# A two-layer hybrid decoder on one core: the compressions' first layer with activations stationary on four column groups

## The chip, the core and the metric
The kernel runs on one NeuronCore of a Trainium2 chip. The metric is the time of one execution in microseconds (us) on the device, everything included from the first load to the last store. Engines are named as the profile names them: PE (TensorE's matmuls), PEld (its weight loads), DVE (VectorE), ACT (ScalarE), POOL (GpSimd) and SP (SyncE, which here only issues DMAs).

## The reference
Two layers run one after the other on 512 tokens of width 1024. Each layer is a half-step SwiGLU, a mixer, a second half-step SwiGLU and a gated input embedding, with layer norms between. The mixer holds three kinds of attention heads side by side. The change is inside one of them, the sparse attention's compression of keys and values:

```python
def compress(kv, pe, w1, w2):
    blk = kv[:, idx] + pe[:, None, :]
    blk = jnp.transpose(blk, (0, 1, 3, 2, 4)).reshape(B, n_cmp, NSA_KV_HEADS, CMP_BLOCK * HEAD_DIM)
    return jax.nn.gelu(blk @ w1) @ w2
```

There are 31 blocks (padded to 32 in the kernel) of 32 tokens by 64 channels, so `blk` is 32 by 2048 and `w1` is 2048 by 256. It is done once for keys and once for values in each layer: four times in all. All of it is float32.

## The kernel before
Big products are made in three passes of a reduced float32 (fp32r): each operand is split into a high part (`whi`, `xh`) and a low part (`wlo`, `xl`), and high by high, low by high and high by low are added in PSUM. A 128x1024 chunk of weights is a "unit": SP loads it as `raw`, ACT copies the high part, DVE or POOL subtracts to get the low part (`_split`, L209 to L219).

The mixer (`mixer`, L423) is written as a list of steps, `SEQ`, of projections (G, q0, q1, kk), score and softmax steps (Q), transposes of the probabilities (T) and products with the values (P). A scheduling layer then places each engine's instructions. So each engine has a fixed order, and an instruction waits only for what it needs.

The steps `cmp`, `hk0` to `hk3`, `hv0` to `hv3`, `ck`, `cv`, `cs`, `ct` are the compression. `g_cmp` (L608) makes `xs`: for keys and for values a tile of 128 partitions, 16 slices of the 2048 inputs and 32 blocks. `phi(i, j)` (L623) is step `hk`j (i = 0) or `hv`j (i = 1); it takes one unit of weights, `wraw`, unsplit, which holds four slices of 128 inputs by 256 outputs. These weights are plain float32. For each slice and each half of the outputs, the weights are the stationary operand (128 columns) and the 32 blocks of `xs` move:

```python
for b in range(4):
    k = 4 * j + b
    for m in range(2):
        self.mm(p[:, 32 * m:32 * m + 32], w[:, b, m], M["X"][:, i, k], k + m == 0, k == 15, True)
```

The result of 16 slices is a 128x64 piece of a PSUM bank `ps` of tag "g". There are two banks of that tag. The bank is taken at j = 0 and is held until DVE has copied it to `gx` (L636). After that come the gelu on DVE (L639 to L647, with one exponential on ACT, L643) and the second layer, `cmp_k` (L653) or `cmp_v`. All matrix products are issued by the helper `mm`, so they all stand at line L249 in the profile; rows are told apart by their tiles. The softmaxes' scores go through two banks of tag "s", and DVE reads each at L732, which is the step that frees the bank.

Of the kernel before, what the change touches and what calls it, by code (L numbers as in the profile page):

```python
# [19 lines left out]
F32 = mybir.dt.float32  # L20
F32R = mybir.dt.float32r
AF = mybir.ActivationFunctionType
# [29 lines left out]
def _mix(w, n):  # L52

    return w.reshape(-1, n, 2, 64 // n).transpose(0, 2, 3, 1).reshape(-1, 128)
# [61 lines left out]
def _consts():  # L116
    c = {}
    c["ident"] = np.eye(128, dtype=np.float32)
    q = np.arange(128)
    m = np.zeros((128, 512), np.float32)  # L120
    m[:, 384:] = np.where(q[None, :] <= q[:, None], 0.0, NEG)
    c["mask"] = m
    ut = np.ones((128, 512), np.float32)
    ut[:, :128] = (q[:, None] <= q[None, :])
    c["ut"] = ut

    def table(d, pos):
        inv = (np.float32(10000.0) ** (-np.arange(0, d, 2, dtype=np.float32) / np.float32(d))).astype(np.float32)
        ang = pos.astype(np.float32)[:, None] * inv[None, :]
        co, si = np.cos(ang).astype(np.float32), np.sin(ang).astype(np.float32)  # L130
        n = 128 // d
        return [np.ascontiguousarray(_mix(np.tile(np.concatenate(x, 1), (1, n)), n).T)
                for x in ((co, co), (-si, si))]

    t = np.arange(S)
    c["rope"] = np.stack([*table(64, t), *table(32, t)])
    be = np.arange(32) * 16 + 31
    c["ropec"] = np.stack(table(64, be), 1)
    ok = (np.arange(32)[None, :] < NCMP) & (be[None, :] <= t[:, None])
    c["maskc"] = np.where(ok, 0.0, NEG).astype(np.float32).reshape(4, 128, 32).transpose(1, 0, 2)  # L140
    c["rowc"] = (t >= 31).astype(np.float32).reshape(4, 128).T
    b = np.zeros((128, 128), np.float32)
    b[:64, :64] = b[64:, 64:] = 1.0 / 64
    c["bd"] = b
    return {k: np.ascontiguousarray(v, np.float32) for k, v in c.items()}


def layout(a):

    a = {k: np.asarray(v) for k, v in a.items()}  # L150
    o = dict(_consts())
    o["x"] = a["x"][0]
    o["xt"] = a["x"][0].T.reshape(KC, 128, S).transpose(1, 0, 2)
    o["pt"] = a["p"][:, 0].transpose(0, 2, 1).reshape(L, 2, 128, S).transpose(0, 2, 1, 3)
    o["ws"] = np.stack(_stream(a, 0) + _stream(a, 1))
    o["ln_g"], o["ln_b"], o["bg"] = a["ln_g"], a["ln_b"], a["ple_b_gate"]
    k2 = a["nsa_phi_k2"].reshape(L, 2, 128, 2, 32)
    o["phik2"] = np.stack([np.repeat(x.reshape(L, 2, 128, 64), 2, 3) for x in (k2, k2[..., ::-1, :])], 3).transpose(0, 2, 1, 3, 4)
    o["phiv2"] = a["nsa_phi_v2"].reshape(L, 2, 128, 64).transpose(0, 2, 1, 3)
    o["pe"] = np.stack([a["nsa_pos_k"], a["nsa_pos_v"]], 1).reshape(L, 2, 16, 128).transpose(0, 3, 1, 2)  # L160
    o["bf"] = a["fox_b_f"]
    o["lam"] = a["diff_lambda"].reshape(L, 128)
    o["sg"] = np.concatenate([a["diff_subln_g"]] * 2, 1)
    return {k: np.ascontiguousarray(v) for k, v in o.items()}
# [3 lines left out]
class _Body:  # L168
# [78 lines left out]
    def mm(self, out, l, r, start, stop, loose=False):  # L247

        self.nc.tensor.matmul(out, l, r, start=start, stop=stop, skip_group_check=loose)  # L249
# [176 lines left out]
    def mixer(self, l):  # L426
        nc, A = self.nc, self.A
# [18 lines left out]
        M = {}  # L446
# [21 lines left out]
        for t in range(NT):  # L468
            p = self.ps("gs"[t % 2])
# [153 lines left out]
        def phi(i, j):  # L623

            if j == 0:
                M["ps", i] = self.ps("g")
            p = M["ps", i][:, 0:64]
            w = self.unit().rearrange("p (b m n) -> p b m n", b=4, m=2)
            for b in range(4):
                k = 4 * j + b  # L630
                for m in range(2):
                    self.mm(p[:, 32 * m:32 * m + 32], w[:, b, m], M["X"][:, i, k], k + m == 0, k == 15, True)
            if j < 3:
                return
            x, y = lw([128, 2, 32], f"gx{i}"), lw([128, 2, 32], f"gy{i}")
            nc.vector.tensor_copy(x, p.rearrange("p (a b) -> p a b", a=2))  # L636

            c = 2.0 * math.sqrt(2.0 / math.pi)
            nc.vector.tensor_mul(y, x, x)  # L639
            nc.vector.tensor_scalar(y, y, -0.044715 * c, -c, op0=ALU.mult, op1=ALU.add)  # L640
            nc.vector.tensor_mul(y, y, x)
            nc.vector.tensor_scalar(y, y, 80.0, None, op0=ALU.min)
            nc.scalar.activation(y, y, AF.Exp)  # L643
            nc.vector.tensor_scalar(y, y, 1.0, None, op0=ALU.add)  # L644
            nc.vector.reciprocal(y, y)
            if i == 0:
                nc.vector.tensor_mul(x, x, y)  # L647
                M["phi", 0] = x
            else:
                g = M["phi", 1] = lw([128, 2, 4, 32], "g1")  # L650
                nc.vector.tensor_mul(g, *(a[:, :, None, :].to_broadcast([128, 2, 4, 32]) for a in (x, y)))
# [225 lines left out]
        for n in SEQ:  # L877
            if n[0] == "h":
                phi("kv".index(n[1]), int(n[2]))
            elif n in steps:  # L880
                steps[n]()
                if len(M) and all(k in M for k in (("q", 0), ("q", 1), "k")) and "n0" not in M:
                    ready()
            else:
                {"G": G, "Q": QS, "T": TP, "P": PV}[n[0]](n[1:])
# [21 lines left out]
        g, b = self.bcast(A["ln_g"][l, 1]), self.bcast(A["ln_b"][l, 1])  # L907
# [55 lines left out]
    def start(self):  # L963
        nc, A = self.nc, self.A

        self.ident = self.cp.tile([128, 128], F32, name="ident")
        self.mhalf = self.cp.tile([128, 1], F32, name="mhalf")
        self.one = self.cp.tile([128, 1], F32, name="one")
        self.eps = self.cp.tile([128, 1], F32, name="eps")
        for n in ("mask", "bd", "maskc", "rowc", "ropec"):  # L970
            setattr(self, n, self.cp.tile(list(A[n].shape), F32, name=n))
        self.xh = self.cp.tile([128, KC, S], F32R, name="xh")
        self.xl = self.cp.tile([128, KC, S], F32R, name="xl")
        nc.vector.memset(self.mhalf, -0.5)
        self.x = [self.h4(F32, name="x") for t in range(NT)]

        z = self.h4(shape=(128, 512), name="zero")
        nc.vector.memset(z.bitcast(F32), 0.0)
        p = self.ps("t")
        for _ in range(self.opt["warm"]):  # L980
            self.mm(p, z[:, 0:128], z, True, True)

        raw = [self.h4(F32, name="raw") for _ in range(2)]
        for u in range(2):
            self.hl[u] = [self.big(self.tags[u], name="w") for _ in range(2)]
        for k in range(KC):
            r = self.big("h", F32, (128, 512), "xraw")
            x = nc.sync.dma_start(r, A["xt"][:, k])
            if k % 2 == 0:
                c = slice(128 * k, 128 * k + 256)  # L990
                for u in range(2):
                    self.last_raw = nc.sync.dma_start(raw[u][:, c], A["ws"][u, :, c])
            self.hilo(self.xh[:, k], self.xl[:, k], r)
            if k % 2 == 0:
                for u in range(2):
                    self.hilo(self.hl[u][0][:, c], self.hl[u][1][:, c], raw[u][:, c])
        self.dma_u = self.split_u = 2
        for u in range(2, 4):
            self._load(u)
            self.after(self.last_raw, x)  # L1000
            self.dma_u += 1
        self.ahead(3)
        nc.vector.memset(self.one, 1.0)
        nc.vector.memset(self.eps, EPS)

    def load_x(self):
        nc, A = self.nc, self.A
        for t, n in ((self.ident, A["ident"]), *((self.x[t], A["x"][128 * t:128 * t + 128]) for t in range(NT)),
                     *((getattr(self, n), A[n]) for n in ("mask", "bd", "maskc", "rowc", "ropec"))):
            self.after(nc.sync.dma_start(t, n), self.last_raw)  # L1010


# [71 lines left out]
```

## Time and profile before

| what | us |
|---|---|
| median of 3 runs | 2188.41 |
| lowest and highest run | 2184.15, 2189.64 |
| the profiled execution, its own time | 2182.96 |
| its span, first to last instruction | 2181.1 |
| PE busy | 2138.7 (98%) |
| PEld busy | 1765.9 (81%) |
| DVE busy | 1049.2 (48%) |
| ACT busy | 819.6 (38%) |
| POOL busy | 152.5 (7%) |

A line of the profile reads: start, duration, engine, line of the kernel, operation, tiles written and read, `rows*columns` of the array, shape, count. Matmuls overlap in a pipeline, so what one costs is the distance from its start to the next one's start, and not its duration. A float32 matmul with no split appears as two MATMUL and two LDWEIGHTS records; one of fp32r as one of each.

### The profile page before, as it was taken

To read this page: it belongs to the slowest core of one execution; us is meant where nothing else is said; L and a number is where in the kernel's file an instruction comes from. 1 tells how busy PE (TensorE), PEld (TensorE's weight loads), DVE (VectorE), ACT (ScalarE), POOL (GpSimd) and SP (SyncE) were. 2 spreads that over 40 slices of the span, in tenths; PEclk is the share of its full clock that TensorE was granted. 3 is DMA by queue.
4 is the path that set the end of the run, shared out by engine and by line. 5 is a ranking of instruction groups with operands and counts; after the bars stand their busy time and mean duration, and the time that the engine had idled before them with its cause. 6 is when DMAs were issued, how large, how long until landed. Compare 5 with 4: busy or idle time off the path is not lost.

```text
span 2181.1 us, 25953 instructions
## 1 busy us (share of the span) xinstructions
PE 2138.7 (98%) x10135; PEld 1765.9 (81%) x10135; DVE 1049.2 (48%) x1777; ACT 819.6 (38%) x1372; POOL 152.5 (7%) x114
## 2 busy tenths in 40 slices
PE   9999999999999999999999999999998999999999
PEld 7888888787778888887888888887877788888887
DVE  4333236378875333334723332363788753333355
ACT  5222213456763222213522222144577532222132
POOL 0000001212210000000000000012212200000000
PEclk9999999989999999999999999999999999999999
DMA  6323334432342323334313333344323413333332
GB/s 202 97 97 97 108 105 152 128 127 92 104 145 66 97 97 97 116 96 136 97 59 97 97 97 106 107 143 136 122 92 110 152 51 96 98 97 118 94 134 68
DMA packets 76107, 236.07 MB, mean 108 GB/s; under 512 B 11344, under 2 KB 13520, under 8 KB 75984
## 3 DMA queue, kind: packets, MB, share of 16 engines
q1 hardware_dynamic: 74864, 230.74, 33.5%
q0 software_dynamic: 1120, 3.67, 0.5%
q8 instruction: 80, 1.31, 0.2%
q14 instruction: 43, 0.35, 0.1%
HBM read 209.46 MB, written 6.29 MB: 99 GB/s over the span
## 4 chain that ended last, share of the span: by engine, by line
PE 89%; DVE 6%; ACT 2%; DMA 1%; issue 1%; SPq 0%; DVEq 0%; ACTq 0%
PE ps L249 86%; PE ps L756 2%; PE ps L266 1%; DMA raw<-in_ws_dram 1%; DVE P L746 1%; DVE P L732 1%; ACT whi L218 1%; DVE PT L242 0%; DVE P L742 0%; DVE wlo L219 0%; DVE raw_r L540 0%; DVE gy L644 0%; DVE pair L797 0%; DMA xraw<-in_xt_dram 0%; DVE xl L269 0%
## 5 line engine op out<-in xcount | busy, mean ns | idle before, releaser
L218 ACT ACTIVATE whi<-raw 128x1024 fp32r<-128x1024 f32 x342 | 361.7, 1060 | 1047.5 <-PE ps L249 678.5
L219 DVE TENSOR_TENSOR wlo<-raw,whi 128x1024 fp32r<-128x1024 f32 x298 | 363.8, 1223 | 609.4 <-ACT whi L218 609.0
L249 PE MATMUL ps<-xh,wlo 128*128 128x512 f32 (+1 forms) x1688 | 644.7, 382 | 0.1
L249 PE MATMUL ps<-xl,whi 128*128 128x512 f32 (+1 forms) x1688 | 644.5, 382 | 0.0
L249 PE MATMUL ps<-xh,whi 128*128 128x512 f32 (+1 forms) x1688 | 643.5, 382 | 0.8 <-ACT xh L268 0.8
L249 PE MATMUL ps<-whi,h 128*128 128x512 f32 x1376 | 430.2, 392 | 0.0
L249 PEld LDWEIGHTS ps<-xh,whi 128*128 128x128 f32 x1688 | 317.2, 188 | 59.9 <-ACT xh L268 1.5
L249 PEld LDWEIGHTS ps<-xh,wlo 128*128 128x128 f32 x1688 | 318.0, 188 | 58.7 <-DVE wlo L219 0.5
L249 PEld LDWEIGHTS ps<-xl,whi 128*128 128x128 f32 x1688 | 317.8, 188 | 58.7 <-DVE xl L269 0.6
L249 PEld LDWEIGHTS ps<-whi,h 128*128 128x128 f32 x1376 | 257.9, 188 | 59.1 <-issue 6.9
L249 PE MATMUL ps<-wlo,h 128*128 128x512 f32 (+1 forms) x704 | 277.5, 394 | 0.0
L335 DVE TENSOR_TENSOR hraw<-silu,ps 128x512 f32<-128x512 f32 x88 | 60.5, 687 | 290.7 <-PE ps L249 289.9
L249 PEld LDWEIGHTS ps<-wlo,h 128*128 128x128 f32 (+1 forms) x704 | 132.0, 188 | 35.3 <-issue 9.6
L219 POOL TENSOR_TENSOR wlo<-raw,whi 128x1024 fp32r<-128x1024 f32 x44 | 107.2, 2437 | 286.2 <-ACT whi L218 208.7
L734 ACT ACTIVATE P<-P,sst 128x128 f32<-128x128 f32 x192 | 106.6, 559 | 26.4 <-DVE sst L732 26.0
L249 PE MATMUL ps<-whi,xh 128*128 128x512 f32 (+2 forms) x264 | 98.9, 377 | 2.0 <-DVE VF L466 2.0
L298 POOL TENSOR_TENSOR mv<-mv,mhalf 128x1 f32<-128x1 f32 x24 | 23.0, 957 | 1111.3 <-DVE mv L297 1111.3
L732 DVE CUSTOM_DVE_ANT_0 P<-ps,mask 128x128 f32<-128x128 f32 x192 | 90.1, 490 | 21.7 <-PE ps L249 20.7
L249 PE MATMUL ps<-wlo,xh 128*128 128x512 f32 (+2 forms) x264 | 98.8, 375 | 0.0
L249 PE MATMUL ps<-whi,xl 128*128 128x512 f32 (+2 forms) x264 | 98.3, 374 | 0.0
L756 PE MATMUL ps<-ident,P 128*128 128x128 f32 x400 | 71.2, 297 | 12.9 <-DVE P L746 9.4
L249 PE MATMUL ps<-whi,oT 128*128 128x512 f32 x256 | 82.6, 395 | 0.0
(194 smaller groups left out, 1928.7 us busy)
## 6 DMA issues: line engine op xcount, KB each, us to landing
raw<-in_ws_dram SPq DMA_DIRECT2D x342, 512.0 KB
wraw<-in_ws_dram SPq DMA_DIRECT2D x16, 512.0 KB
dx<-x SPq DMA_DIRECT2D x8, 512.0 KB
x<-dx SPq DMA_DIRECT2D x8, 512.0 KB
rot<-raw_r SPq DMA_DIRECT2D x28, 128.0 KB
bc<-in_ln_g_dram SPq DMA_DIRECT2D x6, 512.0 KB
bc<-in_ln_b_dram SPq DMA_DIRECT2D x6, 512.0 KB
xraw<-in_xt_dram SPq DMA_DIRECT2D x8, 256.0 KB
```

The lines of the kernel that those rows point to most:

```text
L218: self.nc.scalar.activation(hi, r, AF.Copy)
L219: (self.nc.gpsimd if self.opt["pool"] and tag[1:] else self.nc.vector).tensor_sub(lo, r, hi.bitcast(F32))
L249: self.nc.tensor.matmul(out, l, r, start=start, stop=stop, skip_group_check=loose)
L266: nc.tensor.transpose(p[:, j], self.x[t][:, 128 * k:128 * k + 128], self.ident)
L298: nc.gpsimd.tensor_tensor(mv[:, 3:4], mv[:, 2:3], self.mhalf, op=ALU.pow)
L335: nc.vector.tensor_mul(r[0:n], s[up:up + n], pu[up:up + n])
L732: nc.vector.tensor_tensor_reduce(v, p[:, 0:n], self.mask[:, 512 - n:512], -scale, 3e38, ALU.add, ALU.min, nm[:, t:t + 1])
L734: nc.scalar.activation(v, v, AF.Exp, bias=nm[:, t:t + 1], scale=-1.0, accum_out=sm[:, t:t + 1])
L746: nc.vector.scalar_tensor_tensor(v, v, r[:, t:t + 1], c, op0=ALU.mult, op1=ALU.add)
L756: nc.tensor.transpose(p[:, 128 * i:128 * i + 128], P[:, off[t] + 128 * kb:off[t] + 128 * kb + 128], self.ident)
```

## The change
In `phi`, the operands change places. The 32 blocks of one slice are now the stationary operand (32 columns), and the slice's 128x256 weights move. The four slices of a unit write four groups of 32 PSUM partitions of the same bank, so each uses its own 32 columns of the array. After the last unit there are four partial sums, each 32 blocks by 256 outputs, on top of each other. ACT copies them to SBUF (`qs`), and two float32 matmuls with `four` (four stacked 32x32 identities) as the moving operand add them and turn them to outputs by blocks. From there on, everything is as before. A constant of 128x32 is added and loaded once with the others.

```diff
+    c["four"] = np.tile(np.eye(32, dtype=np.float32), (4, 1))
...
-            p = M["ps", i][:, 0:64]
-            w = self.unit().rearrange("p (b m n) -> p b m n", b=4, m=2)
+            q = M["ps", i][:, 0:256]
+            w = self.unit().rearrange("p (b n) -> p b n", b=4)
+
             for b in range(4):
-                k = 4 * j + b
-                for m in range(2):
-                    self.mm(p[:, 32 * m:32 * m + 32], w[:, b, m], M["X"][:, i, k], k + m == 0, k == 15, True)
+                self.mm(q[32 * b:32 * b + 32], M["X"][:, i, 4 * j + b], w[:, b], j == 0, j == 3, True)
             if j < 3:
                 return
+
+            qs = self.tmp(shape=(128, 256), name="qs")
+            nc.scalar.activation(qs, q, AF.Copy)
+            p = M["ps", i][:, 256:320]
+            for m in range(2):
+                self.mm(p[:, 32 * m:32 * m + 32], qs[:, 128 * m:128 * m + 128], self.four, m == 0, m == 1, True)
             x, y = lw([128, 2, 32], f"gx{i}"), lw([128, 2, 32], f"gy{i}")
...
+        self.four = self.cp.tile([128, 32], F32, name="four")
```

The scheduling layer also moves instructions around these. Lines below the change stand 1 or 6 lines further down in the new program (L249 is L250, L636 is L642).

On PE, where the first units of the keys' compression stand between other heads' work (`ident,P` is a transpose of probabilities, `fb,fa` scores, `PT,VF` a product with values), the order before is:

```order
L249 MATMUL ps<-xs,wraw 128x32 x8
L756 MATMUL ps<-ident,P 128x128 x10
L249 MATMUL ps<-fb,fa 128x128
L249 MATMUL ps<-fa,fb 128x128
L249 MATMUL ps<-fb,fa 128x256
L249 MATMUL ps<-fa,fb 128x256
L249 MATMUL ps<-xs,wraw 128x32 x11
L249 MATMUL ps<-fb,fa 128x384
```

and now:

```order
L250 MATMUL ps<-wraw,xs 32x256 x4
L762 MATMUL ps<-ident,P 128x128 x10
L250 MATMUL ps<-fb,fa 128x128
L250 MATMUL ps<-fa,fb 128x128
L250 MATMUL ps<-fb,fa 128x256
L250 MATMUL ps<-fa,fb 128x256
L250 MATMUL ps<-wraw,xs 32x256 x5
L250 MATMUL ps<-PT,VF 128x512
```

Eight matmuls with 32 moving columns have become four with 256. Over a layer the old ones stand in 18 unbroken runs of PE's order, and the new ones in 12, of 4, 5, 4, 1, 2, 5, 1, 2, 1, 3, 1 and 3.

On PE, where the values' first unit follows the last matmuls of a projection (`xh,whi`, `xl,whi`, `xh,wlo`), the order before is:

```order
L249 MATMUL ps<-xh,wlo 128x512
L249 MATMUL ps<-xs,wraw 128x32 x8
L249 MATMUL ps<-nk,nq 128x128
L249 MATMUL ps<-nkl,nq 128x128
L249 MATMUL ps<-nk,nq 128x256
L249 MATMUL ps<-nkl,nq 128x256
L249 MATMUL ps<-xs,wraw 128x32 x2
L756 MATMUL ps<-ident,P 128x128
```

and now:

```order
L250 MATMUL ps<-four,qs 128x32 x2
L250 MATMUL ps<-xh,whi 128x512
L250 MATMUL ps<-xl,whi 128x512
L250 MATMUL ps<-xh,wlo 128x512
L250 MATMUL ps<-nk,nq 128x128
L250 MATMUL ps<-nkl,nq 128x128
L250 MATMUL ps<-nk,nq 128x256
L250 MATMUL ps<-nkl,nq 128x256
L250 MATMUL ps<-PT,VF 128x512
L250 MATMUL ps<-wraw,xs 32x256 x5
```

The two matmuls that add the keys' parts stand three matmuls ahead of that projection's end, and wait there for ACT's copy; the values' first unit comes behind four scores and a product with values, and waits for DVE's copy to `gx`, which frees the bank.

On DVE, the gelu of the keys (`gx`, `gy`) and what stands around it was, at its second half:

```order
L735 RECIPROCAL sst<-sst 128x4
L640 TENSOR_SCALAR gy_3265<-gy_3265 128x64
L842 TENSOR_TENSOR sst<-sst,sig 128x4
L641 TENSOR_TENSOR gy_3265<-gy_3265,gx_3264 128x64
L742 TENSOR_SCALAR P<-P,sst 128x128
L742 TENSOR_SCALAR P<-P,sst 128x256
L742 TENSOR_SCALAR P<-P,sst 128x384
L742 TENSOR_SCALAR P<-P,sst 128x512
L642 TENSOR_SCALAR gy_3265<-gy_3265 128x64
L242 TENSOR_TENSOR fa<-ps,fa 128x512
L732 ISA P,sst<-ps,mask 128x128
```

and is now:

```order
L642 COPY gx_3254<-ps 128x64
L848 TENSOR_TENSOR sst<-sst,sig 128x4
L243 TENSOR_TENSOR fa<-ps,fa 128x512
L748 TENSOR_SCALAR P<-P,sst 128x128
L748 TENSOR_SCALAR P<-P,sst 128x256
L748 TENSOR_SCALAR P<-P,sst 128x384
L748 TENSOR_SCALAR P<-P,sst 128x512
L645 TENSOR_TENSOR gy_3255<-gx_3254 128x64
L646 TENSOR_SCALAR gy_3255<-gy_3255 128x64
L647 TENSOR_TENSOR gy_3255<-gy_3255,gx_3254 128x64
L648 TENSOR_SCALAR gy_3255<-gy_3255 128x64
L738 ISA P,sst<-ps,mask 128x128
```

The copy to `gx` came 29 rows earlier before; now it stands here, the gelu's first four steps follow in one piece, and the step L644 of before (now L650) comes after the reads of the next two scores, where it stood between them.

## Rows read from the trace of the kernel before

**Rows 1.** The page: busy time of the engines; the chain that ended last.

```profile
PE 2138.7 (98%) x10135; PEld 1765.9 (81%) x10135; DVE 1049.2 (48%) x1777; ACT 819.6 (38%) x1372; POOL 152.5 (7%) x114
...
PE 89%; DVE 6%; ACT 2%; DMA 1%; issue 1%; SPq 0%; DVEq 0%; ACTq 0%
```

**Rows 2.** The answer for the tile xs, both layers (ns least/median/most).

```profile
L249 PEld LDWEIGHTS ps<-xs,wraw x256: 187/192/337, 444.2 to 1576.5; 128*128 128x128 f32 x128
L249 PE MATMUL ps<-xs,wraw x256: 190/276/402, 444.4 to 1576.5; 128*128 128x32 f32 x128
```

**Rows 3.** Timeline of PE: start, us, what, times; runs of the old matmuls.

```profile
444.40 1.86 PE L249 MATMUL ps<-xs,wraw 128*128 128x32 f32 x16
446.10 1.29 PE L756 MATMUL ps<-ident,P 128*128 128x128 f32 x10
...
447.69 2.54 PE L249 MATMUL ps<-xs,wraw 128*128 128x32 f32 x22
450.06 0.42 PE L249 MATMUL ps<-fb,fa 128*128 128x384 f32 x1
```

**Rows 4.** Timeline of PE: float32 with 8 stationary columns and wide moving operand.

```profile
413.41 2.32 PE L249 MATMUL ps<-ut,fz 128*8 128x512 f32 x8
415.66 0.50 PE L249 MATMUL ps<-xh,whi 128*128 128x512 f32 x1
```

**Rows 5.** Timeline of PE: matmuls of 128 and of 64 output columns in turn.

```profile
491.66 1.32 PE L249 MATMUL ps<-PT,VN 128*128 128x512 f32 x8
492.82 0.45 PE L249 MATMUL ps<-xl,whi 128*128 128x512 f32 x1
493.11 0.40 PE L249 MATMUL ps<-xh,wlo 128*128 128x512 f32 x1
493.35 0.39 PE L249 MATMUL ps<-xh,whi 128*128 128x512 f32 x1
```

**Rows 6.** Windows of the compression's stretch, layer one, then layer two.

```profile
core 0: us, PE busy (x) PEld busy (x) DVE busy (x) ACT busy (x) POOL busy (x), PEclk, DMA share, GB/s
446.00:456.00 10.00, 10.00 (x86) 9.70 (x86) 8.37 (x17) 5.75 (x15) 2.37 (x1) 1.00 0.55 187
456.00:464.00 8.00, 8.00 (x45) 6.89 (x43) 7.05 (x28) 6.68 (x21) 0.40 (x1) 1.00 0.62 214
464.00:470.00 6.00, 6.00 (x52) 5.54 (x50) 6.00 (x15) 4.41 (x10) 3.31 (x2) 1.00 0.19 36
470.00:474.00 4.00, 1.57 (x7) 1.19 (x6) 3.97 (x7) 1.49 (x6) 2.43 (x2) 0.87 0.87 276
474.00:487.00 13.00, 13.00 (x55) 12.10 (x54) 6.64 (x26) 5.77 (x19) 0.00 (x0) 0.51 0.03 13
...
1562.00:1575.00 13.00, 13.00 (x64) 12.30 (x64) 7.28 (x28) 7.11 (x22) 0.00 (x0) 0.61 0.04 14
```

**Rows 7.** Timeline of all engines around PE's wait there; last line, PE in layer two.

```profile
469.17 2.37 POOL L219 TENSOR_TENSOR wlo<-raw,whi 128x1024 fp32r<-128x1024 f32 x1 [0.74 <-PE ps L249]
...
469.21 3.27 DVE L644 TENSOR_SCALAR gy<-gy 128x64 f32<-128x64 f32 x1
...
471.51 0.97 DVE L732 CUSTOM_DVE_ANT_0 P<-ps,mask 128x256 f32<-128x256 f32 x1
...
472.57 0.50 PE L249 MATMUL ps<-nk,nq 128*128 128x512 f32 x1 [2.43 <-DVE sst L732]
...
1560.59 0.50 PE L249 MATMUL ps<-nk,nq 128*128 128x512 f32 x1 [2.43 <-DVE sst L732]
```

**Rows 8.** Timeline of DVE: the gelu's same kind of step when POOL rests.

```profile
464.57 0.16 DVE L640 TENSOR_SCALAR gy<-gy 128x64 f32<-128x64 f32 x1
```

**Rows 9.** Timeline of ACT where the copy to qs will stand.

```profile
462.70 0.37 ACT L241 ACTIVATE PT<-ps 128x256 fp32r<-128x256 f32 x1
463.62 0.72 ACT L734 ACTIVATE P<-P,sst 128x512 f32<-128x512 f32 x1 [0.56 <-DVE sst L732]
464.25 0.19 ACT L734 ACTIVATION_READ_ACCUMULATOR P<-P,sst 128x1 f32 x1
```

**Rows 10.** Timeline of PE: the values' first unit follows the projection's end.

```profile
463.80 0.39 PE L249 MATMUL ps<-xh,wlo 128*128 128x512 f32 x1
464.02 1.86 PE L249 MATMUL ps<-xs,wraw 128*128 128x32 f32 x16
```

More of the change, by code (lines that the diff above doesn't have):

```diff
@@ L1008, in load_x @@
         for t, n in ((self.ident, A["ident"]), *((self.x[t], A["x"][128 * t:128 * t + 128]) for t in range(NT)),
-                     *((getattr(self, n), A[n]) for n in ("mask", "bd", "maskc", "rowc", "ropec"))):
+                     *((getattr(self, n), A[n]) for n in ("mask", "bd", "maskc", "rowc", "ropec", "four"))):
             self.after(nc.sync.dma_start(t, n), self.last_raw)
```

## The prediction, made before the changed kernel had run
> **What bounds the kernel now.** Read the page first [rows 1]. PE is busy for 2138.7 of 2181.1 us, and 89% of the chain that ended last is PE. So over the whole kernel PE's time is the time, and a change that takes work from PE should be worth that work. But this change works in one stretch of each layer, so the next view is the table of windows for that stretch [rows 6]. From 446 to 474 us in layer one PE is busy for 25.57 us of 28, and DVE for 25.39 of 28 (sums of the four windows). There both are nearly full, and work taken from PE alone may only make PE wait for DVE. The timeline of that place shows one such wait already: PE stands 2.43 us in each layer for DVE to read scores and free their bank [rows 7]. The next window then shows a granted clock of 0.51 in layer one and 0.61 in layer two [rows 6], so PE spent about all of 13 us, and most of 13 us, on the lower of its two levels (1.2 GHz of 2.4).
>
> **The old matmuls.** There are 128 of them: 2 layers, keys and values, 16 slices, 2 halves. The answer for the tile shows 256 records of each kind, so one float32 matmul is two passes, each with its own weight load [rows 2]. In runs, 16 passes take 446.10 - 444.40 = 1.70 us and 22 take 450.06 - 447.69 = 2.37 us [rows 3]: 0.107 us a pass. Only 32 columns move, but a weight load of 128 columns precedes each pass, and that sets the step. Sum removed: 256 x 0.107 = 27.4 us.
>
> **The new matmuls.** There are 64, so 128 passes with 256 columns moving. The trace has the right neighbour: float32 with 8 stationary columns, four matmuls of 512, 384, 256 and 128 columns, two passes each, 2560 columns in 415.66 - 413.41 = 2.25 us [rows 4]. That is 0.88 ns a column and 0.225 us a pass. One after another, 128 passes take 28.8 us: the upper end, and no gain at all. The gain must come from column groups that run at the same time, and no row shows two groups side by side. If all four ran at once, a run of up to four would take two rounds and one of five four rounds; the 12 runs of a layer then take 28 rounds, so 56 x 0.225 = 12.6 us: the lower end. I take the middle. Both passes of a matmul need the same 32 columns, so the second must follow the first, and in rows 3 to 5 matmuls start in the order of the program. The second pass of one slice can then run beside the first pass of the next, and no more. A run of n takes n + 1 rounds, 44 a layer: 88 x 0.225 = **19.8 us**.
>
> The Trainium skill (TensorE: Matmul & The Clock Gate, Part 3) also says that matmuls start and end strictly in program order; no run here shows it for column groups.
>
> **The sums of the parts.** Eight matmuls with `four` have the old shape (128 stationary columns, 32 moving), so 16 passes x 0.107 = 1.7 us [rows 3]. A change of the array's shape at the ends of runs I cost at nothing: eight matmuls that alternate between 128 and 64 output columns, 2560 columns, take 492.82 - 491.66 = 1.16 us, and uniform neighbours take 493.35 - 493.11 = 0.24 us per 512, which would be 1.20 [rows 5]. The other bound is a pipeline that empties each time: 0.39 us of duration less a step of 0.24 [rows 5] is 0.15 us, at both ends of the 28 runs of the two layers (24 and 4 of `four`): 8.4 us. The row is nearer, since it alternates shapes too; the 8.4 stays in the range.
>
> The Trainium skill (TensorEngine Tiling, Key Properties) says that a change of tiling mode drains TensorE. Rows 5 do not show a drain between 128 and 64 columns; by the page the 8.4 us would be due, and the sum would lie 2.5 us above zero.
>
> ACT's copy to `qs` is four times some 0.4 us, between 0.37 us for 256 columns and 0.72 for an exponential of 512. It falls where ACT idles 0.56 us [rows 9], so I cost the engine nothing; without that gap it would be 1.6 us. The one load of `four` lies with the constants, hundreds of us ahead of its use. On SP one load of a unit is issued behind two small moves; PE's wait in this stretch names DVE and no DMA [rows 7], so nothing.
>
> PE's work: 19.8 + 1.7 - 27.4 = **-5.9 us**, from +3.1 without any overlap to -13.1 with all four.
>
> **What is kept of it.** The keys' units cost 64 x 0.107 = 6.8 us a layer and will cost 21 rounds, 4.7 us. So PE reaches the `four` matmuls up to 2.1 us earlier, and there it meets a wait that is new: ACT's copy stands in ACT's order between a copy and an exponential that wait for DVE [rows 9], and DVE has only 28 - 25.39 = 2.6 us of slack in the whole stretch [rows 6]. Behind `four` stand the rest of the projection and then the values' first unit, which needs the bank that DVE's copy to `gx` frees; before, that unit followed the projection with no wait [rows 10], since `gx` had been copied long ago. I take it that half of the gain is kept: -3 us. The profiled execution took 2182.96 us, so it would take 2180; the median of the runs shown stands 5.4 us above it, so I forecast **2185 us** as a median. A measurement of this kernel tells a change from none at about 0.3%, 6.6 us.
>
> **The rivals.**
> - *The wait behind the gelu goes away.* PE's 2.43 us are DVE's: one step of the gelu on 128x64 took 3.27 us while POOL subtracted a low part for 2.37 us [rows 7]; the same kind of step takes 0.16 us when POOL rests [rows 8]. In the new order that step comes after the reads of two scores, not between them. Then 2 x 2.43 us go, and the slow clock after them: 13 x 0.49 + 13 x 0.39 = 11.4 us [rows 6]. With the 3 us above that is -19.3, so 2169 us. Against it: four scalings of P and two other gelu steps of the same kind now stand just ahead of those reads, and POOL's work still falls there. 17%.
> - *All four groups run at once.* PE's work falls by 13.1 us; with between half and all of it kept, 2175 to 2182. Against it: the two passes of one matmul. The Trainium skill (TensorEngine Tiling, Key Properties) says that different tiles load weights and multiply in parallel, which would give this case; no run here shows it. 8%.
> - *The groups do not overlap.* The change doesn't do what it says: +3.1 us, and 2191.5 us. For it: rows 3 and 4 show one matmul after another whatever the shape. 15%.
> - *The new wait becomes the bound.* The chain PE, ACT (`qs`), PE (`four`), DVE (`gx`), PE (values' first unit) holds PE in its own order, and everything behind it waits too. If it holds PE for more than about 2 us, as the wait in rows 7 did at 2.43, it eats the 5.9 us, adds some 0.5 us of waiting a layer, and is followed by its own stretch at 0.51 to 0.61 of the clock, 11.4 us for both layers [rows 6]: +12.4, so near 2201 us. For it: PE arrives 2.1 us early and DVE is full. Against it: DVE and ACT get some of PE's results earlier as well. 12%.
>
> **How the numbers follow.** The forecast has 48%; of it a fifth falls beyond 0.3% faster, nearly all the rest within. Faster: 10 of the 48, all 17, 6 of the 8, which is 33%. Slower: 9 of the 12 of the new wait, 2 of the 15 and 1 of the 48, which is 12%. Within 0.3%: the other 55%. The range reaches from the first rival's 2169, less 1, to 2197: it takes in no overlap with the emptied pipeline for a part of the runs, and the milder end of the new wait, and leaves out the rest of these two rivals.
>
> **What would show it.** Right: a run of four new matmuls takes 5 x 0.225 = 1.1 us to the next instruction (1.8 without overlap, 0.45 with all four); PE waits up to 2 us at `four` for ACT or at the values' first unit for DVE; the window after PE's wait for scores has a clock near 0.5 still. Wrong: that window at 1.00 (first rival), a second window at 0.5 behind `four` (last rival), or runs of 1.8 us.

## The result, and the profile after

| what | kernel before | changed kernel |
|---|---|---|
| median of the runs taken together, us | 2185.88 (5 runs) | 2212.57 (5 runs) |
| lowest and highest run, us | 2182.75, 2189.64 | 2210.76, 2218.36 |
| span of the profiled execution, us | 2181.1 | 2216.6 |
| mean granted clock | 0.991 | 0.990 |

The ratio is 1.0122, with a 95% interval from 1.0099 to 1.0145. The change made the kernel 26.7 us slower, and the time lies 15.6 us above the upper end of the range that was forecast.

The loss is not where the change is. On the page of the changed kernel, PE is busy 28 us longer than in [rows 1], although it has 112 matmul records fewer (in the last three rows: times, busy us, mean ns of one, idle time ahead and what ended it):

```profile
PE 2167.0 (98%) x10023; PEld 1747.7 (79%) x10023; DVE 1050.6 (47%) x1777; ACT 820.7 (37%) x1376; POOL 151.1 (7%) x114
...
PE 90%; DVE 6%; ACT 2%; issue 1%; DMA 1%; SPq 0%; DVEq 0%; ACTq 0%
...
L250 PE MATMUL ps<-xh,whi 128*128 128x512 f32 (+1 forms) x1688 | 652.5, 387 | 0.8 <-ACT xh L269 0.8
...
L250 PE MATMUL ps<-whi,h 128*128 128x512 f32 x1376 | 430.4, 392 | 0.0
...
L250 PE MATMUL ps<-whi,xh 128*128 128x512 f32 (+2 forms) x264 | 99.8, 380 | 3.7 <-DVE VF L467 3.2
```

The last three rows are from the page's list of the costliest groups. The same three groups of the kernel before:

```profile
L249 PE MATMUL ps<-xh,whi 128*128 128x512 f32 (+1 forms) x1688 | 643.5, 382 | 0.8 <-ACT xh L268 0.8
L249 PE MATMUL ps<-whi,h 128*128 128x512 f32 x1376 | 430.2, 392 | 0.0
...
L249 PE MATMUL ps<-whi,xh 128*128 128x512 f32 (+2 forms) x264 | 98.9, 377 | 2.0 <-DVE VF L466 2.0
```

A row names the moving operand first and the stationary one second. The matmuls in which `xh` or `xl` (the layer norm's output, split in two) moves and the weights are stationary take 5 ns longer each. Those with the two in each other's place, `whi` moving and `xh` stationary, take 3 ns longer. Those in which `whi` moves and `h` (the SwiGLU's hidden activations) is stationary take the same. Nothing in the diff touches any of them. A window of the first SwiGLU, hundreds of us ahead of the compression, shows it best. First the kernel before, then the changed one (columns as in [rows 6]; `x` is the number of instructions):

```profile
60.00:200.00 140.00, 140.00 (x620) 115.92 (x619) 48.39 (x52) 40.90 (x52) 0.00 (x0) 1.00 0.30 98
```

```profile
60.00:200.00 140.00, 140.00 (x605) 113.48 (x604) 46.10 (x49) 39.58 (x51) 0.00 (x0) 1.00 0.29 95
```

PE is busy all the time at full clock, waits for nothing, and issues 605 matmuls of the same shape where it issued 620: a step of 140/605 = 231 ns in place of 226 ns. Over the 3 x 1688 such matmuls that is some 28 us, which is the size of the whole loss.

At the place of the change, the timeline of PE answers to [rows 3] and [rows 10]: a run of four new matmuls (eight passes) and one of five, then the sums with `four`.

```profile
454.38 0.40 PE L250 MATMUL ps<-xh,wlo 128*128 128x512 f32 x1
454.70 0.64 PE L250 MATMUL ps<-wraw,xs 128*32 128x256 f32 x8
455.27 1.31 PE L762 MATMUL ps<-ident,P 128*128 128x128 f32 x10
...
456.98 1.05 PE L250 MATMUL ps<-wraw,xs 128*32 128x256 f32 x10
457.99 0.50 PE L250 MATMUL ps<-PT,VF 128*128 128x512 f32 x1
...
472.07 0.40 PE L250 MATMUL ps<-xh,wlo 128*128 128x512 f32 x1
472.31 0.53 PE L250 MATMUL ps<-four,qs 128*128 128x32 f32 x4
472.67 0.48 PE L250 MATMUL ps<-xh,whi 128*128 128x512 f32 x1
```

The run of four takes 0.57 us and the run of five 1.01 us to the next instruction; the sums take 0.36 us and wait for nothing. So the change does what it says, and better than forecast. The starts of the run of four, one line a pass, show how (us, and ns since the start before):

```
454.378  xh,wlo (the matmul ahead)
454.704  +326   454.711 +7   454.718 +7   454.724 +6
454.944  +220   454.951 +7   454.958 +7   454.964 +6
455.274  +310   ident,P (the matmul behind)
```

The two passes of a lone matmul start 240 ns apart (462.518 and 462.758 us), so the four starts within 20 ns belong to four different matmuls. All four slices start their first pass together, and 220 ns after each its second. Going in costs 326 ns where the step is 230, and going out 310 where it would be 220: some 0.09 us each way.

What answers to [rows 7] stands a little later, in the timelines of DVE, POOL and PE:

```profile
474.89 5.46 DVE L748 TENSOR_SCALAR P<-P,sst 128x128 f32<-128x128 f32 x4
...
490.72 3.13 DVE L748 TENSOR_SCALAR P<-P,sst 128x128 f32<-128x128 f32 x4
```

```profile
475.27 4.79 POOL L220 TENSOR_TENSOR wlo<-raw,whi 128x1024 fp32r<-128x1024 f32 x2 [6.76 <-ACT whi L219]
```

```profile
477.92 0.44 PE L762 MATMUL ps<-ident,P 128*128 128x128 f32 x2 [0.52 <-DVE P L748]
480.40 0.77 PE L762 MATMUL ps<-ident,P 128*128 128x128 f32 x5 [2.04 <-DVE P L748]
...
494.51 0.38 PE L250 MATMUL ps<-nk,nq 128*128 128x256 f32 x1 [1.80 <-DVE sst L738]
```

The wait behind the gelu is gone, as the first rival had it. But the four scalings of P that now stand there meet two of POOL's subtractions and take 5.46 us (2.52 and 2.56 of them for the last two), and PE waits for those instead. The windows that answer to [rows 6] (to PE's first wait, then the slow stretch, and so on):

```profile
474.00:481.60 7.60, 5.04 (x32) 2.26 (x30) 7.10 (x12) 3.46 (x7) 4.79 (x2) 1.00 0.57 135
481.60:485.00 3.40, 3.37 (x14) 3.04 (x14) 3.40 (x13) 1.74 (x7) 0.00 (x0) 0.50 0.32 128
485.00:495.30 10.30, 8.21 (x50) 5.03 (x48) 7.15 (x23) 7.15 (x22) 3.59 (x3) 1.00 0.14 36
495.30:498.70 3.40, 2.86 (x11) 2.55 (x12) 3.30 (x10) 0.76 (x3) 0.00 (x0) 0.50 0.51 206
```

In layer one, two stretches of 3.4 us at a granted clock of 0.50, each behind PE's waits, take the place of one of 13 us. Layer two gains nothing: stretches of 6.8 and 3.4 us at 0.50 (from 1584.1 and from 1601.2 us) stand for one of some 10.

### The profile page after: what moved, and what is told of

It reads as the page before. It is cut to its first block, busy times and chain, and to the rows that moved or that the text cites. A ratio compares the mean times of both kernels' runs of the same rounds, so it can differ in the third digit from the quotient of the medians.

```text
span 2216.6 us, 25735 instructions
## 1 busy us (share of the span) xinstructions
PE 2167.0 (98%) x10023; PEld 1747.7 (79%) x10023; DVE 1050.6 (47%) x1777; ACT 820.7 (37%) x1376; POOL 151.1 (7%) x114
## 4 chain that ended last, share of the span: by engine, by line
PE 90%; DVE 6%; ACT 2%; issue 1%; DMA 1%; SPq 0%; DVEq 0%; ACTq 0%
PE ps L250 87%; PE ps L762 2%; DVE P L748 1%; PE ps L267 1%; DVE P L752 1%; DVE P L738 1%; DVE PT L243 1%; ACT whi L219 0%; DVE raw_r L543 0%; ACT P L740 0%; DVE xl L270 0%; DVE x L304 0%; DVE raw_r L541 0%; DVE osq L813 0%; DVE nkl L243 0%
## 5 line engine op out<-in xcount | busy, mean ns | idle before, releaser
L250 PE MATMUL ps<-xh,whi 128*128 128x512 f32 (+1 forms) x1688 | 652.5, 387 | 0.8 <-ACT xh L269 0.8
L250 PE MATMUL ps<-xl,whi 128*128 128x512 f32 (+1 forms) x1688 | 653.1, 387 | 0.0
L250 PE MATMUL ps<-xh,wlo 128*128 128x512 f32 (+1 forms) x1688 | 653.0, 387 | 0.0
L250 PE MATMUL ps<-whi,h 128*128 128x512 f32 x1376 | 430.4, 392 | 0.0
L250 PEld LDWEIGHTS ps<-xh,whi 128*128 128x128 f32 x1688 | 317.3, 188 | 69.6 <-ACT xh L269 1.5
L250 PEld LDWEIGHTS ps<-xh,wlo 128*128 128x128 f32 x1688 | 318.3, 189 | 67.0
L250 PEld LDWEIGHTS ps<-xl,whi 128*128 128x128 f32 x1688 | 318.3, 189 | 67.0 <-DVE xl L270 0.6
L250 PEld LDWEIGHTS ps<-whi,h 128*128 128x128 f32 x1376 | 257.9, 188 | 59.6 <-issue 6.9
L250 PE MATMUL ps<-wlo,h 128*128 128x512 f32 (+1 forms) x704 | 277.5, 394 | 0.0
L250 PEld LDWEIGHTS ps<-wlo,h 128*128 128x128 f32 (+1 forms) x704 | 132.0, 188 | 35.0 <-issue 9.6
L250 PE MATMUL ps<-whi,xh 128*128 128x512 f32 (+2 forms) x264 | 99.8, 380 | 3.7 <-DVE VF L467 3.2
L250 PE MATMUL ps<-wlo,xh 128*128 128x512 f32 (+2 forms) x264 | 99.7, 379 | 0.0
L250 PE MATMUL ps<-whi,xl 128*128 128x512 f32 (+2 forms) x264 | 99.2, 377 | 0.0
L250 PE MATMUL ps<-whi,oT 128*128 128x512 f32 x256 | 82.5, 395 | 0.0
```

## The experiments

Two questions: what slows matmuls that the change does not touch, and what became of the time that PE saves in the compression.

### A buffer that moves all the others

The compiled program's placement of buffers gives a theory. In the kernel before, `xh` and `xl` lie at bytes 20480 and 36864 of each partition. `four`, 128 bytes wide, was allocated behind `xl`, so every buffer after it (the weights `raw`, `whi`, `wlo`, the activations `h` and all the others) lies 128 bytes further on, with `raw` at 53376 in place of 53248. (20480, 36864 and 53248 are multiples of 512.) The theory: that displacement slows the matmuls. The rival: something that the new instructions do. The kernel before, with an unused tile at that place:

```diff
+        self.pad = self.cp.tile([128, 32], F32, name="pad")
+        nc.vector.memset(self.pad, 0.0)
```

> The kernel before, with an unused tile of 128 bytes a partition at the place where the change puts its constant, so every buffer behind it (weights, probabilities, temporaries) starts 128 bytes further on and nothing else changes but one small memset. Theory 1 (the shift of the buffers makes the gate and up matmuls, activations xh and xl against weights, take 233 ns a step in place of 227): about 25 us more than the kernel before, some 2211 us, and steps of 229 to 238 ns. Theory 2 (the new matmuls, their waits or the new order cost the time): the same as the kernel before within 0.3%, steps of 227 ns.

The changed kernel with `four` in a pool behind all the others, so that nothing moves:

```diff
-        self.four = self.cp.tile([128, 32], F32, name="four")
+        self.four = self.op.tile([128, 32], F32, name="four", tag="four", bufs=1)
```

> The changed kernel, with the constant of 128 bytes placed behind all big buffers, so that these start where they did before the change. Theory 1: the steps of the gate and up matmuls are back at 227 ns and the time falls by about 25 us, to 2180 to 2190 us, near or a little under the kernel before. Theory 2: it stays near 2212 us.

The changed kernel with `four` ahead of `xh`, so that `xh` and `xl` move too, and with `four` 2048 bytes wide:

```diff
+        self.four = self.cp.tile([128, 32], F32, name="four")
         self.xh = self.cp.tile([128, KC, S], F32R, name="xh")
```

> The changed kernel, with the constant ahead of xh and xl, so that xh, xl and all buffers behind move by the same 128 bytes. If the distance between the stationary and the moving operand's addresses counts: back to 227 ns a step and 2180 to 2190 us. If it counts that an operand starts at a multiple of 4096 bytes: still about 233 ns a step and near 2212 us. Theory 2: near 2212 us with 233 ns or not.

```diff
-        self.four = self.cp.tile([128, 32], F32, name="four")
+        self.four = self.cp.tile([128, 512], F32, name="four")[:, 0:32]
```

> The changed kernel, with a constant's tile of 2048 bytes in place of 128, so that the buffers behind it move by 2048 bytes. If only the place within 2048 bytes counts: 227 ns a step and 2180 to 2190 us. If the place within 4096 bytes counts: slower steps again and near 2212 us. Theory 2: near 2212 us.

Two more displacements of the kernel before, 512 and 64 bytes (the tile of the first experiment with 128 and with 16 columns):

> The kernel before with an unused tile of 512 bytes a partition (in place of 128) behind xl, so that every later buffer moves by 512 bytes. If the place of the moving operand counts modulo 512 bytes (the step from one stationary slice of 128 columns to the next), a step of the SwiGLU's gate and up products stays at 227 ns and the time at 2180 to 2190 us. If it counts modulo 2048 bytes (one moving slice of 512 columns), 233 ns and 2212 to 2222 us.

> The kernel before with an unused tile of 64 bytes a partition. If any displacement costs the same, 233 ns a step and 2212 to 2222 us, as with 128 bytes; if the cost grows with the displacement, about half, 230 ns and 2200 us; if a line of 64 bytes or less is what counts, 227 ns and 2180 to 2190 us.

Measured, against runs of the kernel before on the same chip:

| kernel | later buffers against `xh` | median us | ratio and interval | span us |
|---|---|---|---|---|
| before, 128 bytes unused | +128 | 2216.72 | 1.0142 (1.0115 to 1.0169) | 2219.2 |
| change, `four` last | 0 | 2184.57 | 0.9996 (0.9982 to 1.0011) | 2183.7 |
| change, `four` first | 0 (both +128) | 2185.41 | 0.9998 (0.9982 to 1.0014) | 2185.1 |
| change, `four` of 2048 bytes | +2048 | 2186.95 | 1.0013 (0.9999 to 1.0027) | 2185.9 |
| before, 512 bytes unused | +512 | 2186.05 | 1.0025 (0.9983 to 1.0067) | 2187.3 |
| before, 64 bytes unused | +64 | 2198.84 | 1.0102 (1.0063 to 1.0142) | 2197.0 |

The window from 60 to 200 us, for 128 bytes, `four` last, 512 bytes and 64 bytes:

```profile
60.00:200.00 140.00, 140.00 (x604) 113.52 (x603) 47.01 (x51) 39.94 (x52) 0.00 (x0) 1.00 0.30 94
```

```profile
60.00:200.00 140.00, 140.00 (x620) 115.95 (x619) 48.11 (x52) 40.93 (x52) 0.00 (x0) 1.00 0.31 98
```

```profile
60.00:200.00 140.00, 140.00 (x620) 115.91 (x619) 48.02 (x52) 39.64 (x51) 0.00 (x0) 1.00 0.32 98
```

```profile
60.00:200.00 140.00, 140.00 (x602) 112.20 (x601) 46.82 (x51) 39.53 (x50) 0.00 (x0) 1.00 0.30 94
```

The displacement alone makes the whole loss, without any of the change, and without the displacement the loss is gone. It is the distance between the two operands that counts, not the address: with `four` first, both are off by 128 bytes and nothing is lost. `h` is displaced together with the weights, so its matmuls keep their distance, and their time. Whole multiples of 512 bytes, the size of one stationary slice of 128 columns, cost nothing: +512 and +2048. And 64 bytes cost as much a step as 128, so it does not grow with the size. The whole time of the 64-byte kernel (two runs) is lower than that of the 128-byte one all the same, for a reason that the next part uses. What in the memory makes it so, and whether 256 bytes would cost, was not tried.

### Where PE's saved time went

Without the displacement, the change gives 0.9996: nothing. Yet PE has less to do. The mixer of each layer, from the first transposes of its layer norm to the last group norm (`osq,bd`), in windows; first the kernel before, then the change with `four` last:

```profile
364.40:629.70 265.30, 248.39 (x1324) 205.39 (x1322) 192.89 (x484) 165.37 (x385) 60.78 (x41) 0.96 0.37 118
1463.80:1715.90 252.10, 236.00 (x1262) 194.39 (x1262) 182.31 (x467) 159.37 (x376) 55.15 (x37) 0.97 0.37 118
```

```profile
364.70:631.00 266.30, 246.33 (x1267) 194.51 (x1265) 192.74 (x484) 166.04 (x387) 60.50 (x41) 0.96 0.38 118
1466.10:1716.80 250.70, 230.34 (x1205) 179.93 (x1205) 182.04 (x467) 159.90 (x378) 54.57 (x37) 0.98 0.37 119
```

PE is busy 7.7 us less (484.39 against 476.67) and stands idle 7.3 us more (33.0 against 40.3). The answer on what PE waited for between 440 and 530 us (who, for whom: us in total, times, longest), before and with `four` last:

```profile
PE ps L249 <- DVE sst L732: 4.3, 2, 2.4
PE ps L712 <- DVE sc L705: 1.0, 1, 1.0
```

```profile
PE ps L250 <- DVE sst L738: 5.0, 4, 1.8
PE ps L762 <- DVE P L748: 2.6, 2, 2.0
PE ps L698 <- ACT scr L695: 0.8, 1, 0.8
```

Theory A was that the scalings that POOL stretches hold up what PE gained. Theory B was that the waits follow whatever order comes out, so that what is taken from PE at one place comes back as a wait at another. The scaling was put on ACT, in the kernel before and in the change with `four` last:

```diff
-                    (nc.gpsimd if t in self.opt["npool"] else nc.vector).tensor_scalar(
-                        v, v, r[:, t:t + 1], None, op0=ALU.mult)
+                    nc.scalar.activation(v, v, AF.Copy, scale=r[:, t:t + 1])
```

> The kernel before, with the scaling of the probabilities (four steps a softmax) on ACT in place of DVE, and nothing of the change. Theory A (the change's saved PE time is given back at waits for these scalings, which take 5.45 and 3.13 us in place of 1.27 when POOL subtracts a low part at the same time): the kernel before has its 2.43 us wait at a gelu step and not at a scaling, so little changes here, 2175 to 2188 us. Theory B (whatever PE gains in that stretch it gives back at the next wait, since DVE's work as a whole sets the time there): DVE loses some 1.3 us a softmax, and this kernel and its partner with the change gain alike.

> The change with its constant allocated last (so that no other buffer moves), and the scaling of the probabilities on ACT. Theory A: the waits of 2.21, 1.95 and 0.99 us a layer go, and some of the slow clock behind them, so 8 to 15 us below the partner without the change: 2165 to 2175 us. Theory B: within 0.3% of the partner without the change.

Before: 2191.15 us, 1.0062 (1.0034 to 1.0090). Change: 2192.89 us, 1.0078 (1.0047 to 1.0108). Theory A in this form falls: DVE's work was lightened by some 20 to 28 us over the kernel, and neither got faster. The scheduling layer made another order of it, with waits of 2.1 to 2.9 us at other places, so this was no clean test of the one wait.

Next, the other side of the collision. Two of POOL's subtractions were given to DVE, in both kernels, and then the first of them alone. `DVE_LO` is a set that the kernel has for this, empty so far:

```diff
-DVE_LO = ()
+DVE_LO = ("Gd0", "Gf2")
```

> The kernel before, with the low parts of two projections' weights (Gd0 and Gf2) subtracted on DVE in place of POOL; these are the two subtractions that POOL makes near 465 to 471 us in layer one. Theory A (PE's gain is held up by DVE steps that POOL's subtractions stretch): the wait of 2.6 us a layer and the slow clock behind it go, 2170 to 2180 us. Theory B (the waits follow whatever order comes out, and what is taken away at one place comes back at another): within 0.3% of the kernel before.

> The change with its constant allocated last, and the same two subtractions on DVE. Theory A: the wait of 2.2 us a layer behind the scaling that took 5.45 us goes, and the 10 us less of PE work show up against the partner without the change: 8 us or more below it, 2160 to 2172 us. Theory B: within 0.3% of the partner without the change.

```diff
-DVE_LO = ()
+DVE_LO = ("Gd0",)
```

> As lo_new, with only the first of the two subtractions on DVE; its order of work differs from the change's (constant last) in one stretch of some 30 us a layer alone. Theory A: half of the stretched scaling goes, 2 to 4 us a layer, 2176 to 2181 us. Theory B: within 0.3% of the change with its constant last, 2178 to 2191 us.

> The kernel before, with the subtraction for Gd0 alone on DVE, the partner of lo_new_one. If the 10 us less of PE work are what lo_new_one shows, this one stays within 0.3% of the kernel before, 2176 to 2189 us, and some 8 us above lo_new_one. If moving that subtraction is the gain and the change has no part in it, it is level with lo_new_one, 2170 to 2177 us. It may also be slower than before, since the order that comes out differs over most of the mixer.

| edit | kernel before | change, `four` last | one by the other |
|---|---|---|---|
| none | 1 | 0.9996 (0.9982 to 1.0011) | 0.9996 |
| scalings on ACT | 1.0062 (1.0034 to 1.0090) | 1.0078 (1.0047 to 1.0108) | 1.0016 |
| `Gd0`, `Gf2` on DVE | 1.0028 (1.0011 to 1.0044) | 1.0046 (1.0029 to 1.0062) | 1.0018 |
| `Gd0` on DVE | 1.0031 (1.0014 to 1.0048) | 0.9977 (0.9961 to 0.9992) | 0.9946 |

The ratios are all against the kernel before of the same chip. In three orders out of four, theory B holds: what is taken from PE changes nothing that 0.3% would show. In the fourth it comes out, and more: 2174.75 us (2171.22 to 2180.72) against 2189.16 for the partner without the change, which ran on another chip (the kernel before took 2180.20 us on the one and 2182.35 on the other). That is below what either theory expected. This is the only kernel of the study that is faster than the kernel before, by 0.23%, and the span of its profiled execution is 2169.4 us. Its mixers, and then its partner's:

```profile
365.40:622.10 256.70, 239.43 (x1267) 187.88 (x1265) 191.11 (x485) 165.41 (x387) 57.69 (x40) 0.99 0.39 122
1458.10:1704.10 246.00, 230.62 (x1205) 178.70 (x1205) 179.60 (x468) 159.83 (x378) 52.46 (x35) 0.98 0.39 121
```

```profile
365.30:631.50 266.20, 246.48 (x1323) 203.06 (x1321) 188.36 (x485) 164.99 (x385) 58.95 (x40) 0.96 0.37 118
1465.50:1720.30 254.80, 236.02 (x1261) 193.34 (x1261) 177.82 (x468) 159.16 (x376) 53.56 (x36) 0.96 0.37 117
```

The two mixers together can be split in three: PE's idle time, what the lower clock adds while PE is busy (summed over windows of 1 us by their granted clock), and the rest, which is PE's work at full clock.

| kernel | both mixers, us | idle | lower clock | the rest |
|---|---|---|---|---|
| before | 517.4 | 33.0 | 18.5 | 465.9 |
| change, `four` last | 517.0 | 40.3 | 16.6 | 460.1 |
| before, `Gd0` on DVE | 521.0 | 38.5 | 16.3 | 466.1 |
| change, `four` last, `Gd0` on DVE | 502.7 | 32.7 | 8.4 | 461.7 |

The work falls by 5.8 and 4.4 us. What decides is the other two columns, and they swing by 7 and by 10 us with the order. Each row is one profiled execution, and the best kernel's is the fastest of its ten runs (2171.22 us), so the last row flatters it. In that execution PE's waits stay short there (1.12 us at most from 462 to 482 us), and from 440 to 500 us the clock is 1.00, where the kernel before had 0.51 for 13 us [rows 6]:

```profile
471.61 0.44 PE L250 MATMUL ps<-nk,nq 128*128 128x384 f32 x1 [1.12 <-DVE sst L738]
...
440.00:500.00 60.00, 55.86 (x328) 40.85 (x327) 49.38 (x144) 37.84 (x97) 12.35 (x9) 1.00 0.44 139
```

How little it takes is seen in the kernels with 64 and with 128 unused bytes. Their instructions stand in the same order as in the kernel before. With 128 bytes the gelu step of [rows 7] takes 3.27 us again; with 64 bytes it reads, in the timelines of POOL and DVE:

```profile
477.96 2.44 POOL L219 TENSOR_TENSOR wlo<-raw,whi 128x1024 fp32r<-128x1024 f32 x1 [0.77 <-PE ps L249]
```

```profile
477.97 0.18 DVE L644 TENSOR_SCALAR gy<-gy 128x64 f32<-128x64 f32 x1
```

In [rows 7] DVE's step comes 40 ns after POOL's start and takes 3.27 us; here it comes 10 ns after and takes 0.18. The records, to the ns, say it of both layers: 39 and 44 ns after POOL's start in the kernel before, 26 and 26 with 128 bytes, 43 and 43 with 512, and 3.26 to 3.28 us each time; 6 and 5 ns with 64 bytes, and 0.18 us. The 3.27 us are not POOL's subtraction alone. The next row of POOL, of the kernel before, shows a memset right behind it:

```profile
471.48 0.96 POOL L664 MEMSET kp<- 128x1024 f32 x1
```

It ends at 472.44 us, and DVE's step 0.04 us later: the step is held through both of POOL's instructions. The gap between the starts does not say by itself which of the two is held. In the kernel before with the scalings on ACT, the same step starts 50 and 54 ns ahead of POOL's subtraction and still takes 2.50 and 2.52 us. What decides it was not tried.

In the kernel with 64 bytes PE's 2.43 us are gone, and so is the slow stretch behind them:

```profile
470.00:487.00 17.00, 16.33 (x118) 14.90 (x117) 15.96 (x49) 12.79 (x40) 5.83 (x3) 1.00 0.35 98
1575.00:1592.00 17.00, 16.34 (x111) 14.65 (x110) 15.17 (x41) 9.06 (x28) 6.06 (x5) 1.00 0.30 93
```

The two mixers take 509.1 us there, and 527.8 with 128 bytes, though the matmuls step alike. PE's idle time makes 4.2 us of the 18.7, and its busy time (479.77 and 494.23 us) the rest: with 128 bytes a stretch at the lower clock follows the wait in each layer. So in these two executions such meetings went with some 19 us, three times the change's own 6; no run holds all else still. The kernel with 512 bytes, with one order of instructions, shows a spread of that size from run to run: its five runs took from 2169.83 us, at a mean granted clock of 0.995, to 2195.93, at 0.986. What its faster runs met is not on record, since one run of each kernel is profiled.

## Why the prediction was wrong

**The step that failed** is the one that put the constant at nothing: "The one load of `four` lies with the constants, hundreds of us ahead of its use". SP does issue that load early (at 32.4 us), and with `four` last, where it is loaded as well, nothing is lost. The place of the buffer is what costs: its 128 bytes behind `xl` move all later buffers against `xh` and `xl`, every matmul between them takes 231 ns in place of 226, and that is the whole of the 26.7 us lost. No rival had it, since the argument priced instructions and never places. With `four` last the same change measures 2184.57 us, next to the 2185 of the forecast. That is luck: the forecast stood 3 us below its kernel before, at 2188.41, and this kernel is level with the kernel before of its own chip, at 2183.33. PE's work fell by as much as was forecast and none of it was kept, where half was to be.

**The new matmuls** were mis-sized: 19.8 us from overlap by pairs, on the ground that matmuls start in the order of the program, with both passes of one ahead of the next. They don't: the passes of four matmuls interleave, a run of four takes 0.57 us where 1.1 was expected, and the lower bound of 56 rounds holds: 56 x 0.22 = 12.3 us. The rival of all four at once, given 8%, was the right mechanism. The rule on program order that was weighed there (the Trainium skill, TensorE: Matmul & The Clock Gate, Part 3) does not put both passes of one matmul ahead of the next one's here: the starts above interleave. In which order the compiled program holds the passes the trace does not show, so the rule itself is neither borne out nor refuted.

**The change of the array's shape** was costed at nothing from [rows 5] and does cost: 0.09 us in and 0.09 out, 24 runs, 4.3 us. That is between the two bounds of zero and 8.4 (which counted the four runs of `four` too, whose shape is their neighbours'). The Trainium skill (TensorEngine Tiling, Key Properties) says that a change of tiling mode drains TensorE, and that different tiles work in parallel; both agree with the starts of the run of four, though no run takes the 0.09 us apart. The alternation of 128 and 64 columns in [rows 5] was not the same case. Together, 12.3 + 4.3 is 16.6 us; with `four` last the 24 runs add up to 15.1 us from their starts to the next instruction (without a wait of some 0.3 us in one of them), and 17.3 with the way in.

**The old matmuls** were mis-sized too: 27.4 us takes every pass at the pace of the long runs, but 20 of the 36 runs have only two or four passes, and two take 0.14 us to the next instruction (from 451.19 to 451.33 us in the kernel before). From start to next start the 36 runs add up to some 25.6 us, with the four that fell on the lower clock counted at half. The sums with `four` take 0.36 or 0.42 us each, 1.6 in all.

**PE's work**, forecast at -5.9 us, is 17.3 + 1.6 - 25.6 = -6.7 by these steps, so the errors nearly cancel. The balance of the mixers has -5.8 and -4.4. The difference of one to two us stays open.

**What is kept of it** was to be half, 3 us; with `four` last it is none. The wait was sought at `four`, where there is none (0.36 us for four passes, close to the step in [rows 3]), and at the values' first unit, where there is none either. It came at the transposes of P, 0.52 and 2.04 us, and at the next scores, 1.80 us. The first rival's own counter-argument named that mechanism: "four scalings of P and two other gelu steps of the same kind now stand just ahead of those reads, and POOL's work still falls there". Its chance of 17% was for the wait behind the gelu to go, and it went; that its time would be 2169 took for granted that none follows. An order in which only short ones follow exists, and there the median is 2174.75 us.

**The last rival**, at 2201, expected the new wait and the lower clock to add 12.4 us to the time. With `four` last the waits add 7.3 us to PE's idle time, and the lower clock adds no more than before (16.6 against 18.5 us); together they eat what PE saves and no more.

## What to carry to other kernels

A new tile has a price besides its load: when a kernel's inner matmuls read two buffers, compare their distance before and after, and put small late constants behind everything, or keep what is inserted to a multiple of the stationary slice (512 bytes here). When work that nobody touched slows by 2% at full clock and without waits, look at addresses first. And where two engines hold each other up by turns, a few us taken from one show up only in an order that lets them through; test the same edit in two or three orders before it is judged, with several runs of each.

## What was not expected of the hardware

- A matmul with 128 stationary and 512 moving columns takes 226 ns or 231 to 233 ns to the next one, with the same instruction and clock, by the distance of its two operands in a partition: 64 and 128 bytes more cost it, 0, 512 and 2048 don't.
- Four float32 matmuls on four groups of 32 columns start 7 ns apart, and their second passes 220 ns later, again 7 ns apart; a lone one takes 0.55 us to the next instruction, four take 0.57.
- A DVE step on 128x64 took 0.18 us where it started 5 or 6 ns after POOL's subtraction, and 3.27 us, to the end of the memset behind that subtraction, where it started 26 to 44 ns after. The four scalings of P take 1.27 us when POOL rests (at 470.67 us in the changed kernel) and 5.46 us beside two subtractions. The Trainium skill (Advanced Engine Details and Errata, GPSIMD Details) has POOL share a read and a write interface with DVE, in conflict with some kinds of DVE instruction. The rows agree, with 3.27 us for a step that is caught behind POOL's 2.37 and 0.96.
